# Attention in-projection of a hybrid attention and convolution block: chunk by chunk, or in pairs by Strassen's seven products

## The chip, the core and the metric

The kernel runs on one core of a Trainium2 chip. The metric is the device time of one execution in microseconds (us); lower is better. The times given are medians of several executions. Traces are taken by the hardware profiler on one execution. Engines are called as the profile calls them: PE (TensorE, matrix products; PEld its weight loads), DVE (VectorE), ACT (ScalarE), POOL (GpSimd), SP (SyncE, which here only issues transfers).

## What is computed

Two layers over 1024 latent tokens of width 1024, with a context of 256 tokens; everything is fp32. Layer 0 is attention, layer 1 a convolution module, and a final RMS norm follows. The change is in layer 0 alone:

```python
h = modulate(rmsnorm(x), shift, scale)             # (1024 tokens, 1024); h_ctx likewise (256, 1024)
proj = h @ w_in                                    # w_in (1024, 5120)
q = apply_rope(split_heads(proj[..., :2048], 16))  # 16 query heads of 128
k = apply_rope(split_heads(proj[..., 2048:2560], 4))
v = split_heads(proj[..., 2560:3072], 4)           # 4 key and value heads
z = proj[..., 3072:]                               # gate, 16 x 128
kv_c = h_ctx @ w_in[:, 2048:3072]                  # context keys and values
o = windowed_attention(q, k, v, kc, vc, sink)      # |i-j| <= 128, plus all context keys, one softmax
x = x + gate * ((o * silu(z)) @ w_out)
```

## The kernel before

**Products of split numbers.** An fp32 operand is split in a high part that TensorE's fast fp32 form takes (`F32R`; an ACT copy makes it) and a low part, the rest (one subtraction, `split_lo`, on DVE or POOL). Each product is three matmuls: high with high, high with low, low with high. Activations `Hh`, `Hl` hold the transposed `h` in 8 pages of 128 x 1024 each (8 blocks of 128 input channels, 1024 tokens). A weight chunk is 128 output columns of `w_in`, so one head of q, k, v or z: `wraw` (512 KB) is loaded, ACT makes `whi`, DVE or POOL makes `wlo`.

**The fill.** A chunk is 2 halves of 512 tokens x 8 channel blocks x 3 = 48 matmuls of 512 columns, into a bank `psg` (`gemm_half`). In the attention stage these are the fill between the attention's own matmuls. The stage goes through 128 steps: 16 heads h of 8 query blocks qb of 128 tokens. A step issues on PE the scores of the next block (6 matmuls into `pss`), `FILL = 12` fill matmuls, at some steps a product with the values (`pv`, into `pso`), and the transposes of the block's probabilities (`pss<-ident,p`). The softmax goes DVE (mask and maximum, a custom instruction), ACT (exp), DVE (reciprocal), POOL (scaling) and back to PE's transposes; ACT and DVE then split the transposed block into `pthi` and `ptlo`. Chunks for z and q are made one head ahead; every fourth head `job(("k", g))` and `job(("v", g))` run as a whole between two heads. Each chunk's result is finished by ACT, DVE and POOL: q and k by rotary positions (`rope`: copy out, swap halves by two transfers, two products and a sum, split), v by transposes and a split, z by tanh and a product.

**Beside it.** DVE also adds up the modulation rows of the second layer (`ada_rest`: `dww_raw`, `wsum_raw`, 128 transfers of 128 KB). `low_parts` makes the low parts of both output weights (ACT `lhi`, POOL `low`) and keeps them in DRAM (`wolA`, `wolC`); the projection after the attention (`proj_attn`, 32 steps of a 512 KB weight piece) loads `wo` and `wolA`.

**What sets the order.** PE goes in program order (`pin("P")`). The order on DVE, ACT, POOL and SP is set by the scheduler from priorities and its own estimate of times; each engine then runs its list in order, so that an instruction that waits holds all behind it. Transfers are issued by SP, the two of a rope swap by ACT; eight semaphores for transfers are used in turn, so that a transfer may wait for the one eight before it. Memory is 45 pages of 4 KB per partition and 6 halves of 528 words.

All instructions pass through one helper, so that every row of the trace has line L89 (after the change L144); tiles tell them apart.

```python
        for kt in range(KT):                       # gemm_half: one half of the tokens of one chunk
            PE.matmul(o, wh[:, kt], Hh[kt][:, sl], start=kt == 0, stop=False)
            yield
            PE.matmul(o, wh[:, kt], Hl[kt][:, sl], start=False, stop=False)
            yield
            PE.matmul(o, wl[:, kt], Hh[kt][:, sl], start=False, stop=kt == KT - 1)
            yield
...
        if nxt and not regroup:                    # a step of the attention stage
            scores(*nxt)
...
            fill(n)
        if pvq:
            pv(*pvq.popleft())
...
        transposes(h, qb)
```

Of the kernel before, what the change touches and what calls it, by code (L numbers as in the profile page):

```python
# [2 lines left out]

# [30 lines left out]
FILL = 12  # L34
# [42 lines left out]


# [16 lines left out]
def backbone_kernel(  # L95
# [19 lines left out]
    pg = Pages(pgpool, 45, "page", 1024)  # L115
    hp = Pages(hfpool, 6, "half", 528)

# [162 lines left out]
    for key, src in (("k", 0), wk[0]), (("q", 0), wcol(0)), (("v", 0), wv[0]):  # L280
        add_chunk(key, src)
    for h in range(NH):
        add_chunk(("z", h), wcol(AW + 2 * KW + h * P))
        if h + 1 < NH:
            add_chunk(("q", h + 1), wcol((h + 1) * P))
        if h % 4 == 3 and h + 1 < NH:
            add_chunk(("k", h // 4 + 1), wk[h // 4 + 1])
            add_chunk(("v", h // 4 + 1), wv[h // 4 + 1])
    wsA = WStream(chunks, nraw=4, lo_eng=lambda i: V if i < 4 else G)
# [375 lines left out]
    def ada_rest():  # L665
# [8 lines left out]
        bank = ps_o(1)  # L674
        acc, o = bank[:, 0:256], bank[:, 256:512]
        for i, (l, c0, kt) in enumerate(todo):
# [11 lines left out]
            yield  # L688
            if kt < KT - 1:
                continue  # L690
            V.tensor_copy(acc_a, acc)
            yield "copied"
            if i + 1 == len(todo):
                yield
            if c0 >= 2048:
                PE.matmul(o[0:1], ones[:, 0:1], acc_a, start=True, stop=True)
                V.tensor_copy(acc_a[0:1], o[0:1])
                SY.dma_start(out=gd[l][:, c0 - 2048:c0 - 1792], in_=acc_a[0:1])
            else:
                for b in range(2):  # L700
                    PE.matmul(o[:, b:b + 1], acc_a[:, b * P:b * P + P], ones[:, 0:1], start=True, stop=True)
                V.tensor_copy(mod1[:, c0 // P:c0 // P + 2], o[:, 0:2])

# [6 lines left out]
    wolA, wolC = (dr.tile([2, NK, P, 2, 512], F32, tag=n, name=n) for n in ("wolA", "wolC"))  # L710
# [5 lines left out]
    made = []  # L716

    def store():
        while made:
            dst, raw = made.pop()  # L720
            SY.dma_start(out=dst, in_=raw)
            pg.free(raw)

    def low_parts():

        items = [(pair_rows(w, m, kk), d[m, kk]) for w, d in ((Wo, wolA), (Wp, wolC)) for m in range(2) for kk in range(NK)]
        his = pg.alloc(F32R, [2, 512], "lhi")
        raws = {}

        def load(i):  # L730
            if i < len(items):
                raws[i] = pg.alloc(F32, [2, 512], "low")
                SY.dma_start(out=raws[i], in_=items[i][0])

        for i, (_, dst) in enumerate(items):
            load(i)
            raw = raws.pop(i)
            store()
            yield "open"
            for b in range(2):  # L740
                after(act(his[:, b], raw[:, b], AF.Copy), anchor_a)
                after(split_lo(G, raw[:, b], raw[:, b], his[:, b]), anchor_p)
                if b == 0:
                    yield "open"
            made.append((dst, raw))
            yield "shut"
        store()
        pg.free(his)
# [5 lines left out]
    def proj_attn():  # L754
# [4 lines left out]
        def load(i):  # L759
            s, kk = seqB[i]  # L760
            h, m = subs[s]
            w, wl = pg.alloc(F32, [2, 512], "wo"), pg.alloc(F32R, [2, 512], "wol")
            SY.dma_start(out=w, in_=pair_rows(Wo, m, kk))
            SY.dma_start(out=wl.bitcast(F32), in_=wolA[m, kk])
            st[i] = [w, wl]
# [5 lines left out]
        def split(i):  # L771
            s, kk = seqB[i]
            h, m = subs[s]
            w, wl = st[i]
            wh = pg.alloc(F32R, [2, 512], "woh")
            if i:
                act(wh, w, AF.Copy)
            else:
                V.tensor_copy(wh, w)
            pg.free(w)  # L780
# [135 lines left out]
    def early_proj():  # L916
        pg.free(*Hh, *Hl, cos, sin)
        for v in projA:
            if v == "early":
                break  # L920
            yield

    kvt = {}
    qt = {}
    zt = {}
# [12 lines left out]
    def rope(o, sl, d, ropes=None, hold=None, eng=G):  # L938
        qe, qs = (hp.alloc(F32, None, "rope") for _ in range(2))
        m = (hp if ropes is None else pg).alloc(F32, None, "rope")  # L940
        e, w, r = qe[:, 0:512], qs[:, 0:512], m[:, 0:512]
        act(e, o, AF.Copy)
        queue = A if ropes is None else SY
        queue.dma_start(out=w[0:64], in_=e[64:128])
        queue.dma_start(out=w[64:128], in_=e[0:64])
        first = tt(V, r, o, cos[:, sl], ALU.mult)
        if ropes is None:
            tt(G, w, w, sin[:, sl], ALU.mult)

        def sine():  # L950
            tt(V, w, w, sin[:, sl], ALU.mult)
            tt(V, r, r, w, ALU.add)

        def high_low():
            act(d[0][:, sl], r, AF.Copy)
            low()

        def add(behind=None):
            i = tt(eng if ropes is None and hold is None else V, r, r, w, ALU.add)
            if behind:  # L960
                after(i, [behind])
            act(d[0][:, sl], r, AF.Copy)

        def low():
            split_lo(eng if ropes is None else V, d[1][:, sl], r, d[0][:, sl])
            hp.free(qe, qs)
            (hp if ropes is None else pg).free(m)
# [1008 lines left out]
```

## Time and profile before

| | |
|---|---|
| time, median of 3 executions | 1686.36 us (1686.04 to 1686.93) |
| span of the profiled execution, first to last instruction | 1684.8 us, 1.6 us under the median; its own time is taken as the span and these 1.6 us |
| instructions | 23963 |
| PE / DVE / ACT / POOL busy | 1675.0 / 1116.1 / 878.8 / 871.0 us |
| attention stage, from the first softmax to the early output projection | 75 us to about 795 us |
| convolution layer and end | from about 960 us |
| transfers | 244.55 MB, 145 GB/s in the mean |

How to read it: "busy" is time in which an engine has an instruction of the program in work; matmuls overlap their ends, so that a busy PE says that it was never without one, and how long one matmul keeps the next from starting is read from the distance of two starts. A row of a table of stretches gives, for a window of the span, the busy time and the number of instructions of each engine, the granted clock, the mean share in which the 16 transfer engines were busy, and GB/s. A row of a group gives count, busy time, mean length of one in ns, the idle time ahead of them and what ended it.

### The profile page before, as it was taken

How to read it: one execution, taken by the hardware profiler on the slowest of the kernel's cores; microseconds unless marked ns; L12 is line 12 of the kernel's file. 1: busy time of each engine (PE TensorE's matmuls, PEld its weight loads, DVE VectorE, ACT ScalarE, POOL GpSimd, SP SyncE). 2: the span in 40 equal slices, each digit the busy share in tenths (PEclk: the TensorE clock that was granted, in tenths of full speed). 3: DMA queues.
4: the chain of work that ended last, by engine and by line, in shares of the span. 5: the costliest groups of instructions: out<-in, count | busy, mean ns of one | idle time of the engine just before them, and what ended most of it. 6: DMA issues, size and time to landing. Idle time of an engine off the chain costs nothing.

```text
span 1684.8 us, 23963 instructions
## 1 busy us (share of the span) xinstructions
PE 1675.0 (99%) x8436; PEld 1413.9 (84%) x8436; DVE 1116.1 (66%) x2131; ACT 878.8 (52%) x1555; POOL 871.0 (52%) x722
## 2 busy tenths in 40 slices
PE   9999999999999999999999999999999999999998
PEld 6888888888888888888888888888888888888886
DVE  5765654566356644566324289999999999868732
ACT  5745543555355543556334365555665654566741
POOL 0256653666366663653001267999898888130400
PEclk9999999999999999999999999999999999999999
DMA  9424443454244443447976522020211202387881
GB/s 387 150 85 153 134 121 95 153 153 141 84 152 144 143 135 98 135 135 251 320 233 228 213 94 91 11 72 17 75 51 51 82 33 80 130 276 241 310 298 50
DMA packets 114776, 244.55 MB, mean 145 GB/s; under 512 B 11626, under 2 KB 36514, under 8 KB 114656
## 3 DMA queue, kind: packets, MB, share of 16 engines
q1 hardware_dynamic: 108576, 233.06, 40.9%
q10 hardware_dynamic: 6080, 9.97, 2.4%
q8 instruction: 66, 1.08, 0.3%
q14 instruction: 54, 0.44, 0.1%
HBM read 190.80 MB, written 41.69 MB: 138 GB/s over the span
## 4 chain that ended last, share of the span: by engine, by line
PE 98%; DVE 0%; DMA 0%; ACT 0%; POOL 0%; issue 0%; ACTq 0%; POOLq 0%
PE psg L89 51%; PE pss L89 26%; PE pso L89 22%; DMA rope_half<-rope_half 0%; POOL rope_half L89 0%; DVE x_page L89 0%; ACT p_page L89 0%; DVE wlo_page L89 0%; ACT pthi L89 0%; ACT rope_half L89 0%; ACT whi_page L89 0%; DVE hf_page L89 0%; DVE hl_page L89 0%; ACT qh_page L89 0%; ACT lhi_page L89 0%
## 5 line engine op out<-in xcount | busy, mean ns | idle before, releaser
L89 POOL TENSOR_TENSOR odd_half<-odd_half,prod_half 128x513 f32<-128x513 f32 (+2 forms) x252 | 314.7, 1257 | 22.6 <-ACT prod_half L89 9.4
L89 POOL TENSOR_TENSOR wlo_page<-wraw_page,whi_page 128x512 fp32r<-128x512 f32 (+1 forms) x104 | 173.0, 1680 | 186.7 <-DVE ql_page L89 72.0
L89 PE MATMUL psg<-hh_page,whi_page 128*128 128x512 f32 x600 | 236.3, 394 | 0.0
L89 PE MATMUL psg<-hl_page,whi_page 128*128 128x512 f32 x600 | 234.4, 391 | 0.0
L89 PE MATMUL psg<-hh_page,wlo_page 128*128 128x512 f32 x600 | 234.0, 390 | 0.0
L89 ACT ACTIVATE prod_half<-ubuf,dww 128x513 f32<-128x513 f32 (+2 forms) x252 | 165.6, 675 | 116.9 <-POOL odd_half L89 113.0
L89 PE MATMUL psg<-h2h_page,whi_page 128*128 128x512 f32 x464 | 181.9, 392 | 0.0
L89 PE MATMUL psg<-h2h_page,wlo_page 128*128 128x512 f32 x464 | 180.6, 389 | 0.0
L89 PE MATMUL psg<-h2l_page,whi_page 128*128 128x512 f32 x464 | 180.6, 389 | 0.0
L89 POOL TENSOR_SCALAR p_page<-p_page,sc 128x640 f32<-128x640 f32 (+1 forms) x128 | 99.6, 779 | 149.5 <-DVE sc L89 131.8
L89 DVE SCALAR_TENSOR_TENSOR pss<-ubuf,dww,pss 128x512 f32<-128x512 f32 (+3 forms) x270 | 172.4, 670 | 0.1
L89 DVE SCALAR_TENSOR_TENSOR pss<-ubuf,wsum,pss 128x512 f32<-128x512 f32 (+3 forms) x270 | 171.7, 671 | 0.2
L89 ACT ACTIVATE p_page<-p_page,sc 128x641 f32<-128x641 f32 (+1 forms) x128 | 102.9, 804 | 98.3 <-DVE sc L89 95.9
L89 ACT ACTIVATE pthi<-pss 128x512 fp32r<-128x512 f32 (+2 forms) x144 | 87.3, 618 | 109.7 <-PE pss L89 99.8
L89 DVE TENSOR_TENSOR ptlo<-pss,pthi 128x512 fp32r<-128x512 f32 (+2 forms) x144 | 101.8, 716 | 61.2 <-ACT pthi L89 59.9
L89 PEld LDWEIGHTS psg<-hh_page,wlo_page 128*128 128x128 f32 x600 | 112.7, 188 | 24.3
L89 PEld LDWEIGHTS psg<-hh_page,whi_page 128*128 128x128 f32 x600 | 112.8, 188 | 19.2 <-ACT hh_page L89 0.3
L89 PEld LDWEIGHTS psg<-hl_page,whi_page 128*128 128x128 f32 x600 | 112.8, 188 | 18.4
L89 ACT ACTIVATE whi_page<-wraw_page 128x1024 fp32r<-128x1024 f32 x88 | 92.6, 1052 | 49.8 <-PE psg L89 21.1
L89 PE MATMUL pso<-h2h_page,whi_page 128*128 128x512 f32 x304 | 118.3, 389 | 0.0
L89 PE MATMUL pso<-h2h_page,wlo_page 128*128 128x512 f32 x304 | 118.3, 389 | 0.0
L89 PE MATMUL pso<-h2l_page,whi_page 128*128 128x512 f32 x304 | 118.3, 389 | 0.0
(262 smaller groups left out, 3992.4 us busy)
## 6 DMA issues: line engine op xcount, KB each, us to landing
wraw_page<-in_k_wconv_dram SPq DMA_DIRECT2D x48, 512.0 KB, 3.3
wraw_page<-in_k_win_dram SPq DMA_DIRECT2D x40, 512.0 KB, 3.6
wo_page<-in_attn_w_out_dram SPq DMA_DIRECT2D x32, 512.0 KB, 6.2
wol_page<-wolA SPq DMA_DIRECT2D x32, 512.0 KB, 8.3
wo_page<-in_conv_w_out_dram SPq DMA_DIRECT2D x32, 512.0 KB, 6.7
wol_page<-wolC SPq DMA_DIRECT2D x32, 512.0 KB, 6.2
rope_half<-rope_half ACTq DMA_DIRECT2D x76, 128.0 KB, 2.4
araw_page<-in_k_ada_dram SPq DMA_DIRECT2D x16, 512.0 KB, 10.1
```

Of the source, the lines that this page charges most:

```text
L89: r = f(*a, **k)
```

## The change

36 of the 40 chunks are now made in 18 pairs (`pairs`: q and z of heads 1 to 15, k and v of groups 1 to 3; q, k, v and z of head or group 0 stay as they were). For a pair, the 1024 channels are two halves, the 1024 tokens two halves, and the two chunks the two column halves of a 2 x 2 block product, which Strassen's scheme (Winograd's form) makes with seven block products in place of eight: 7 x 4 channel blocks x 3 = 84 matmuls in place of 96. For it

- the activations' block sums S1 to S4 are made once, in head 0, by DVE, POOL and ACT (`sums`). S3 takes the place of the block of tokens 512 to 1023 in channels 0 to 511 in `Hh`, `Hl`; S4 stays in memory (`s4`); S1 and S2 go to DRAM (`sd`) and are streamed in for each pair, 8 loads of 512 KB (`sw`, from `stream`, each issued as PE has used the block that it replaces);
- the weights' block sums are made for each pair by DVE: 4 subtractions of 128 x 512; high parts are 7 ACT copies, low parts 7 subtractions, 3 on DVE (`PAIR_V`) and 4 on POOL;
- the products go to three banks (`psg`, `pso`, `psg`) that the pairs share; ACT copies one of them to start the next sum (`pso<-psg`) and two out, and 4 DVE sums put the results together. Of one of the halves q's or k's input now comes from memory and not from PSUM; the gate of both halves and the cosine product likewise.

With it the surroundings move: gates go to DRAM and back (`zd`), keys and values of groups 1 to 3 too (`kd`, `vd`, `cd`), so that no chunk is made as a whole between two heads; the context's chunks are all made in head 0; cosine and sine are loaded anew for each half (`k_cos`, `k_sin`); q is allocated by halves; `ada_rest` adds up in memory and not in PSUM. `low_parts` makes only `wolC`; `proj_attn` makes the low parts of its weights itself, by POOL (`wol<-wo,woh`). Small transfers and splits are put off by a count of fill matmuls (`soon`), and `quota` says how many fill matmuls lie behind each step: 258 in head 0, then 14, 13.1, 13.1 and 10.5 a step in the four groups.

```diff
-FILL = 12
+KEPT = 12
+ROPE_AT = 12
+HEAD0 = (30, 36, 36, 36, 36, 28, 28, 28)
+PAIR_V = (1, 4, 6)
...
-    wsA = WStream(chunks, nraw=4, lo_eng=lambda i: V if i < 4 else G)
+    wsA = WStream(chunks, nraw=4, lo_eng=lambda i: V if i < 4 or i % 2 else G)
...
+        def halves(self, src, i, b, then=None):
+            t = pw[0].alloc(F32R, [2, 512], "whl")
+            act(t[:, 0], src, AF.Copy)
+            def low():
+                split_lo(V if b in PAIR_V else G, t[:, 1], src, t[:, 0])
...
+            if b == 0:
+                self.halves(r1[:, 0], i, b)
+                self.t[i] = t = pw[0].alloc(F32, [2, 512], "wt")
+                tt(V, t[:, 0], r2[:, 1], r2[:, 0], ALU.subtract)
+            elif b == 1:
+                t = self.t[i]
+                self.halves(t[:, 0], i, b)
+                tt(V, r2[:, 0], r2[:, 0], r1[:, 0], ALU.subtract)
+                tt(V, t[:, 1], r2[:, 1], r2[:, 0], ALU.subtract)
+            elif b == 2:
+                self.halves(r1[:, 1], i, b)
+                tt(V, r1[:, 0], r1[:, 1], self.t[i][:, 1], ALU.subtract)
...
+    ORDER = ("A11", "S3", "A12", "S2", "A22", "S4", "S1")
+    STREAM = ("S2", "S1")
+    def sums(k):
+        f, g = (pg.alloc(F32, [2, 512], "sf") for _ in range(2))
+        for t, i, eng in ((f, k, V), (g, k + 4, G)):
+            tt(eng, t.rearrange("p a b -> p (a b)"), Hh[i].bitcast(F32), Hl[i].bitcast(F32), ALU.add)
+        yield
+        tt(V, g[:, 1], f[:, 1], g[:, 1], ALU.add)
+        tt(V, f[:, 1], f[:, 0], f[:, 1], ALU.subtract)
+        tt(V, f[:, 0], g[:, 1], f[:, 0], ALU.subtract)
+        tt(V, g[:, 0], g[:, 0], f[:, 0], ALU.subtract)
...
+        for n, src in (("S3", f[:, 1]), ("S2", f[:, 0]), ("S4", g[:, 0]), ("S1", g[:, 1])):
+            hi, lo = dst[n]
+            split_lo(G if n == "S1" else V, lo, src, hi)
...
+    def job_pair(i):
...
+        for b, n in enumerate(ORDER):
+            bank, first = ((a_, True), (c_, True), (a_, False), (b_, False), (a_, True), (b_, False), (c_, True))[b]
+            w = wsP.need(7 * i + b)
+            for k in range(4):
+                ah, al = hblock(n, k)
+                for p, (x, y) in enumerate(((w[0], ah), (w[0], al), (w[1], ah))):
+                    PE.matmul(bank, x[:, k], y, start=first and k == 0 and p == 0, stop=k == 3 and p == 2,
+                              skip_group_check=not first)
+                    yield
+                hdone(i, n, k)
...
+            if b == 0 and i:
+                act(b_, a_, AF.Copy)
+            if b == 1:
+                act(zs, c_, AF.Copy)
+            if b == 3:
+                tt(V, zs, b_, zs, ALU.add)
+            if b == 4:
+                tt(V, e, a_, zs, ALU.add)
+        act(e0, c_, AF.Copy)
+        tt(V, e1, e0, zs, ALU.add)
+        tt(V, e0, b_, e0, ALU.add)
```

**PE, in a step of head 1.** Of the kernel before, the fill: one chunk (`whi`, `wlo`) with the activations' pages, at the end of one half of the tokens and the start of the other.

```order
L89 MATMUL psg_1455<-hh_page_546,whi_page_1339 128x512
L89 MATMUL psg_1455<-hl_page_547,whi_page_1339 128x512
L89 MATMUL psg_1455<-hh_page_546,wlo_page_1340 128x512
L89 MATMUL psg_1551<-hh_page_268,whi_page_1339 128x512
L89 MATMUL psg_1551<-hl_page_269,whi_page_1339 128x512
L89 MATMUL psg_1551<-hh_page_268,wlo_page_1340 128x512
```

Of the changed kernel, from the last row of a score product: the streamed block sums S2 with the weights of one product (`whl` holds its high and its low part), and the next product.

```order
L144 MATMUL pss_2281<-kvc_page_616,q_page_1942 128x256
L144 MATMUL pso_1482<-sw_page_2079,whl_page_2173 128x512 x3
L144 MATMUL pso_1482<-sw_page_2111,whl_page_2173 128x512 x3
L144 MATMUL psg_1481<-hh_page_410,whl_page_2189 128x512
L144 MATMUL psg_1481<-hl_page_411,whl_page_2189 128x512
L144 MATMUL psg_1481<-hh_page_410,whl_page_2189 128x512
L144 MATMUL psg_1481<-hh_page_449,whl_page_2189 128x512
```

A matmul of the fill has the same shape as before, and there are fewer; some now read what a transfer has just brought, and all read weights that were made for one product.

**DVE, in head 0, ahead of the third softmax.** Of the kernel before, between two softmax instructions (`ISA p_page`), with the two evictions of the first block's results:

```order
L89 ISA p_page_959,sc_960<-pss_952,mask_page_597,nsink 128x640
L89 ISA sc_960 128x1
L89 TENSOR_TENSOR rope_half_899<-pss_621,cos_page_560 128x512
L89 SCALAR_TENSOR_TENSOR zs_page_915<-zs_page_915,psg_918 128x512
L89 RECIPROCAL sc_960<-sc_960 128x1
L89 TENSOR_TENSOR ptlo<-pss_988,pthi 128x4x128
L89 SCALAR_TENSOR_TENSOR pso_945<-dww_raw,cs,pso_945 128x256
```

Of the changed kernel, the same place:

```order
L144 ISA p_959,sc_960<-pss_952,mask_page_597,nsink 128x640
L144 ISA sc_960 128x1
L144 TENSOR_TENSOR wlo_page_1034<-wraw_page_972,whi_page_1033 128x1024
L144 TENSOR_TENSOR sf_page_1198<-hh_page_343,hl_page_344 128x1024
L144 TENSOR_TENSOR hl_page_269<-sf_page_1044,hh_page_268 128x512
L144 RECIPROCAL sc_960<-sc_960 128x1
L144 SCALAR_TENSOR_TENSOR zs_half_979<-zs_half_979,psg_919 128x512
L144 TENSOR_TENSOR sf_page_1105<-hh_page_300,hl_page_301 128x1024
L144 TENSOR_TENSOR wlo_page_1167<-wraw_page_1040,whi_page_1166 128x1024
```

The block sums (`sf`, and S3's low part into `hl`) and the context weights' low parts (`wlo`) now stand between the softmax's instructions; all of them have two inputs in memory.

**SP, in the middle of the attention.** Of the kernel before:

```order
L89 DMA wsum_raw<-in_ada_w_dram 128x256
L89 DMA ozd<-oz_half_1374 128x384
L89 DMA dww_raw<-in_ada_w_dram 128x256
L89 DMA low_page_1508<-in_attn_w_out_dram 128x2x512
L89 DMA wsum_raw<-in_ada_w_dram 128x256
L89 DMA dww_raw<-in_ada_w_dram 128x256
L89 DMA wolA<-low_page_1387 128x1024
```

Of the changed kernel:

```order
L144 DMA sw_page_5501<-sd 128x1024
L144 DMA wsum_raw<-in_ada_w_dram 128x256
L144 DMA rope_half_5423<-oz_page_5312 64x512 x2
L144 DMA ozd<-oz_page_5460 128x384
L144 DMA sw_page_5513<-sd 128x1024
L144 DMA sw_page_5547<-sd 128x1024
L144 DMA sw_page_5552<-sd 128x1024
L144 DMA cos_page_5715<-in_k_cos_dram 128x512
L144 DMA cos_page_5715<-in_k_sin_dram 128x512
```

The stream's blocks (`sw`), the swaps of late halves (`rope`, 64 partitions each), cosine and sine now stand in SP's list with the modulation rows and the stores; in all SP's list has 1022 transfers, before 654.

721 lines of the change are left out of this document (499 added, 222 removed).

## Prediction

> **What bounds the kernel now.** I read the page's busy times and the chain that ended last first, then a table of stretches for the stage that the change touches, then PE's own timeline there.
>
> ```profile
> span 1684.8 us, 23963 instructions
> PE 1675.0 (99%) x8436; PEld 1413.9 (84%) x8436; DVE 1116.1 (66%) x2131; ACT 878.8 (52%) x1555; POOL 871.0 (52%) x722
> PE 98%; DVE 0%; DMA 0%; ACT 0%; POOL 0%; issue 0%; ACTq 0%; POOLq 0%
> ```
>
> PE is never without a matmul but for 9.8 us, and 98% of the chain is its. So what counts is how long matmuls keep each other from starting, and whether anything new makes PE wait. The stretches (columns: PE, PEld, DVE, ACT, POOL busy, granted clock, share of the transfer engines, GB/s), the attention stage first, then one group of four heads (heads 4 to 7), then three stretches with heavy transfers:
>
> ```profile
> 75.00:795.00 720.00, 719.90 (x4001) 627.08 (x4000) 402.98 (x898) 361.92 (x774) 401.95 (x366) 1.00 0.43 134
> 264.30:452.70 188.40, 188.40 (x1056) 165.50 (x1056) 103.89 (x230) 93.67 (x201) 108.75 (x98) 1.00 0.44 133
> 800.00:900.00 100.00, 100.00 (x464) 82.83 (x463) 31.58 (x69) 33.27 (x48) 6.48 (x13) 1.00 0.81 280
> 810.00:850.00 40.00, 40.00 (x189) 32.83 (x188) 8.66 (x20) 15.29 (x20) 3.53 (x10) 1.00 0.95 332
> 820.00:840.00 20.00, 20.00 (x90) 16.58 (x89) 5.34 (x9) 7.96 (x12) 2.51 (x2) 1.00 1.00 376
> ```
>
> In 720 us of attention stage PE idles 0.1 us, DVE is 56% busy, ACT 50%, POOL 56%, transfers 43%: PE alone is the bound, and each other engine has room. The price of a fill matmul is the distance of starts, not the 390 ns that a group's mean shows. One step's fill of twelve, first and last, and the transpose behind:
>
> ```profile
> 301.09 0.40 PE L89 MATMUL psg<-hh_page,whi_page 128*128 128x512 f32 x1
> ...
> 303.61 0.39 PE L89 MATMUL psg<-hh_page,wlo_page 128*128 128x512 f32 x1
> 303.84 0.27 PE L89 MATMUL pss<-ident,p_page 128*128 128x128 f32 x1
> ```
>
> Twelve take 303.84 - 301.09 = 2.75 us, 0.229 us each.
>
> **The change, part by part.**
>
> *PE.* 18 pairs lose 12 matmuls each, 216; one added to clear a bank: 215 x 0.229 = 49.2 us. All else on PE keeps its count and shapes. Without a wait the stage takes 671 us in place of 720, and the whole span 1635.6; with the 1.6 us around it 1637.2, set against the median of 1686.4. The rest of this part asks what fills up meanwhile.
>
> The prices on the other engines:
>
> ```profile
> L89 DVE TENSOR_TENSOR rope_half<-psg,cos_page 128x512 f32<-128x512 f32 x36 | 24.8, 690 | 23.1 <-ACT rope_half L89 22.0 <-ACT p_page L89 0.8
> L89 DVE TENSOR_TENSOR rope_half<-rope_half,rope_half x9: 679/693/1769, 238.4 to 624.5; 128x512 f32<-128x512 f32 x9
> L89 DVE TENSOR_TENSOR rope_half<-rope_half,rope_half 128x512 f32<-128x512 f32 x9 | 9.4, 1047 | 14.0 <-POOL rope_half L89 14.0
> 15.52 1.22 DVE L89 TENSOR_TENSOR wlo_page<-wraw_page,whi_page 128x1024 fp32r<-128x1024 f32 x1
> L89 POOL TENSOR_TENSOR wlo_page<-wraw_page,whi_page 128x512 fp32r<-128x512 f32 x72 | 93.1, 1315 | 120.3 <-DVE ql_page L89 72.0 <-PE pso L89 18.6 <-ACT whi_page L89 16.8
> L89 ACT ACTIVATE lhi_page<-low_page 128x512 fp32r<-128x512 f32 x64 | 40.1, 626 | 0.0
> L89 ACT ACTIVATE rope_half<-psg 128x512 f32<-128x512 f32 x36 | 21.3, 591 | 18.7 <-PE psg L89 18.3
> L89 ACT ACTIVATE whi_page<-wraw_page 128x1024 fp32r<-128x1024 f32 x88 | 92.6, 1052 | 49.8 <-PE psg L89 21.1 <-issue 12.9 <-DMA wraw_page<-in_k_win_dram 6.7
> ```
>
> A 128 x 512 operation of DVE takes 0.69 us, if one input is in PSUM always; with both in memory the nine rope sums have a median of 693 ns, a mean of 1047 and a maximum of 1769. The long ones began under a POOL operation:
>
> ```profile
> 248.71 2.99 POOL L89 TENSOR_TENSOR wlo_page<-wraw_page,whi_page 128x512 fp32r<-128x512 f32 x2
> 248.79 1.76 DVE L89 TENSOR_TENSOR rope_half<-rope_half,rope_half 128x512 f32<-128x512 f32 x1 [0.26 <-POOL rope_half L89]
> ```
>
> DVE started 0.08 us behind POOL's first subtraction and ended after 1.76 us in place of 0.69; POOL's two took 2.99 in place of 2 x 1.315. [...]
>
> *DVE.* Per pair 4 weight differences, 3 low parts and 4 output sums: 11 x 0.69 = 7.6 us, 137 in 18 pairs. The block sums: 4 x (one of 1024 at 1.22 and seven of 512) = 24. Three more context low parts of 1024, 4. Less 12 special rope operations and 16 copies, 15. 403 + 150 = 553 of 671 us, 82%. New with both inputs in memory are, per pair, 7 of the weights, one sum, two gates, two cosine products, 12; with the block sums' 28 and the three, 247. At the mean of 1047 they add 247 x 0.354 = 87: 640 us, 95%. DVE then has room on the average and hardly any in a stretch.
>
> *POOL* gives up 66 weight low parts and 32 of the output weights' and takes 72 low parts and 8 block sum operations (four of double width): 402 - 87 - 42 + 95 + 16 = 384, 57%; that pays for itself. *ACT*: 126 high parts at 0.63 for 36 chunks at 1.05, 41 more; 54 bank copies at 0.6, 32 more; 16 sums, 10; less 32 `lhi`, 18 rope copies and 16 gate copies, 37: 408, 61%. No cost, with the room that POOL and ACT have, unless they stand behind a late DVE.
>
> *Transfers.* Stream 144 x 0.52 MB = 75.5, its stores 4, gates out and in 19, cosine and sine 17, keys, values and context 16, less `low` and `wolA` of the first output weight 17: 115 MB on the 96 of the stage (720 us x 134 GB/s), 211 MB in 671 us, 315 GB/s. A group of four heads (188.4 us now, about 169 without five pairs' 60 matmuls and the context chunk) needs 56 MB by SP's list, 330 GB/s. That is the rate of 810 to 850, where the engines were 0.95 busy and PE never waited; 820 to 840 shows 376 at 1.00. A streamed block is asked for 36 fill matmuls ahead, about three steps of 5 us; landings were
>
> ```profile
> wraw_page<-in_k_win_dram SPq DMA_DIRECT2D x40, 512.0 KB, 3.6
> wol_page<-wolA SPq DMA_DIRECT2D x32, 512.0 KB, 8.3
> ```
>
> 3.6 us in the light attention stage and 8.3 in the heavy one behind it. 15 us cover 8.3; a kv pair's stretch (25 MB in 68 us, 370 GB/s) uses the reserve up. Bounds 0 and, at 332 GB/s, 25 / 0.332 - 68 = 7 us in each of three regroups, 22. I take 4, nearer the 376 row.
>
> ```profile
> 289.45 0.28 PE L89 MATMUL pso<-pthi,vh_page 128*128 128x256 f32 x1
> 289.56 0.28 PE L89 MATMUL pso<-ptlo,vh_page 128*128 128x256 f32 x1
> 289.68 0.28 PE L89 MATMUL pso<-pthi,vl_page 128*128 128x256 f32 x1
> ```
>
> *Head 0.* Here the block sums, the context's six chunks and the first weights meet. From the first softmax of head 0 to the low part of the second product's weights DVE's list has 84 operations: 37 with two inputs in memory (31 x 0.69 + 6 x 1.22 = 28.7) and 47 others, 22: 51 us, to 64 if the 37 cost 0.354 more each. PE has 42.5 us there: 66 matmuls at 0.229, 168 of 256 columns at 0.12 (the distance of the starts below), and 60 small ones for the rest. PE must wait for that low part: 51 less overlapping ends is 48, so 5 us at least, 21 at most. With POOL busy for just over half of that time I take 10.
>
> *The other heads.* The softmax of a step goes through DVE, ACT, DVE, POOL, and PE needs it a step later:
>
> ```profile
> 333.53 0.87 DVE L89 CUSTOM_DVE_ANT_0 p_page<-pss,mask_page,nsink 128x640 f32<-128x640 f32 x1
> 336.51 0.80 POOL L89 TENSOR_SCALAR p_page<-p_page,sc 128x640 f32<-128x640 f32 x1
> 339.38 0.71 PE L89 MATMUL pss<-ident,p_page 128*128 128x128 f32 x5
> ```
>
> POOL ended at 337.31, PE asked at 339.38: 2.1 us to spare at 55% DVE. Behind one DVE operation that is blocked (1.07 us more) the room holds; behind two it doesn't. Bounds 0 and 2 us a head; with 82 to 95% busy and room of 2 us I take 0.5 in each of 15 heads, 7.
>
> *The output projection.* The `wol` loads go, and POOL makes 62 subtractions of 1.3 us where it has 6.48 of 100 us busy (800 to 900). Per weight piece 1.05 + 2 x 1.3 = 3.7 us against 24 matmuls, 5.5. PE did not wait for transfers there, so nothing is gained; 0 to 5, taken as 0.
>
> *Sum:* -49 + 10 + 7 + 4 = -28 on a span of 1684.8: 1656.8, and 1658.4 as time.
>
> **Rivals.**
>
> *PE stays full.* DVE's list in head 0 starts early enough, everything else is hidden: 1637 to 1643. For it, a stretch of the convolution layer in which DVE is 98% busy and POOL 87% and PE misses nothing; against it, the 51 us of DVE beside 42.5 of PE in head 0, of which 5 must show.
>
> ```profile
> 1200.00:1400.00 200.00, 200.00 (x884) 165.62 (x883) 195.65 (x279) 119.19 (x158) 173.46 (x120) 1.00 0.17 58
> ```
>
> *DVE becomes the bound because POOL shuts it out.* With a mean of 0.693 + (671 - 553) / 247 = 1.17 us per two-input operation DVE fills the stage, and 1.37 eats the whole gain; at the largest value, 1.77, DVE needs 553 + 247 x 1.08 = 820 us, time 1786. The nine rows' mean, 1.05, stands just below the point, with POOL about as busy as it will be. [...]
>
> *Transfers set the pace (slower).* SP's list is one queue, with half as many transfers again; one that waits for PE or DVE holds the stream's loads behind it, and PE then waits for `sw`. It decides at 211 MB / 720 us = 293 GB/s: below that nothing is won. 800 to 900 ran at 280, with engines at 0.81; at that rate the stage takes 754 us, time 1720. Against it: nothing there asked for more.
>
> **How the numbers follow.** About 0.2% (3.4 us) can be told from no change: 1683.0 to 1689.8 counts as the same. The forecast (1643 to 1680) has 0.58; PE full 0.18; DVE shut out, from 1680 on, 0.11 (0.03 faster, 0.02 the same, 0.06 slower); transfers 0.13 (0.03, 0.03, 0.07). Faster 0.82, same 0.05, slower 0.13. The likeliest gives 1658; 8 in 10 lie between 1639 (nearly nothing waits) and 1690.
>
> **What would show it.** PE with about 8220 instructions and 12 to 40 us of idle time; waits of PE's `pso` in head 0 for DVE or POOL `whl`; DVE 1240 to 1350 us busy, its two-input operations at a mean of 0.8 to 1.1; POOL near 935, ACT near 925; 345 MB moved, 300 GB/s or more in the stage; nothing changed from the convolution on. PE waits for `sw` loads above 20 us, or for POOL's probabilities in each head, would prove me wrong on the slow side; no idle PE in head 0 on the fast side.

## The result: 6.9% slower, and the profile after

| | before | after |
|---|---|---|
| time, median of 4 executions | 1686.64 us | 1802.44 us |
| ratio, 95% interval | | 1.0687 (1.0672 to 1.0702) |
| span of the profiled execution | 1684.8 us | 1800.3 us |
| PE without a matmul | 9.8 us | 118.0 us |
| mean granted clock | 0.999 | 0.972 |

The head of the page and the chain that ended last:

```profile
span 1800.3 us, 24912 instructions
PE 1682.3 (93%) x8221; PEld 1400.5 (78%) x8221; DVE 1374.4 (76%) x2337; ACT 919.4 (51%) x1649; POOL 1012.5 (56%) x778
PE 62%; DVE 14%; DMA 13%; issue 4%; POOL 2%; ACT 2%; SPq 1%; ACTq 0%; DVEq 0%; POOLq 0%
```

215 matmuls are gone, as forecast, and the span grew by 115.5 us. PE's busy time is 1682.3 us where 1675.0 - 49.2 = 1625.8 were to be expected, 56.5 too much; its idle time is 108.2 above that of before: -49.2 + 56.5 + 108.2 = 115.5. The same columns as in the prediction, first the whole attention stage, then head 0, then the rest of it:

```profile
75.85:910.00 834.15, 734.83 (x3822) 621.18 (x3823) 648.34 (x1106) 404.56 (x878) 474.01 (x371) 0.94 0.78 257
78.80:168.00 89.20, 69.08 (x372) 60.09 (x371) 73.64 (x105) 38.89 (x80) 50.32 (x33) 0.84 0.62 214
168.00:910.00 742.00, 664.18 (x3446) 559.73 (x3445) 572.63 (x1000) 362.98 (x793) 420.74 (x337) 0.95 0.80 263
```

The loss lies in the attention stage: 834 us in place of 720, from 910 us on the kernel takes what it took. PE idles 20 us in head 0 and 78 in the other fifteen heads, 5.2 each in the mean. No engine is full: DVE is busy 78% of the stage, POOL 57%, ACT 48%, the transfer engines 78% at 257 GB/s. The largest of PE's waits over the whole span (in total, how often, longest):

```profile
PE pso L144 <- DVE ptlo L144: 16.4, 12, 4.0
PE pss L144 <- DVE ptlo L144: 11.6, 14, 3.6
PE pss L144 <- ACT q_page L144: 9.8, 4, 6.5
PE pss L144 <- POOL p L144: 9.5, 6, 2.9
PE pss L144 <- DVE sc L144: 9.0, 14, 1.5
```

Most are small. Somewhat under half of the 110 us that the view lists, 51 us with 4.2 for `pthi`, ends with a part of the softmax (`sc`, `p`, `pthi`, `ptlo`); the rest is scattered over q, gates and sums, and none is for a streamed block `sw`. Three waits are longer than 6 us, 19 us together, and all end with ACT: for q (6.5), for the copy of a bank (6.6) and for weights (`whl`, 6.1). They are not the softmax's. Ahead of the longest, the copy stood in ACT's list behind two others, and ACT itself had waited 2.43 us for POOL.

**One of the softmax's waits.** DVE, POOL and PE around 401 us:

```profile
400.87 1.75 DVE L144 TENSOR_TENSOR whl_page<-wt_page,whl_page 128x512 fp32r<-128x512 f32 x1
402.55 1.75 DVE L144 TENSOR_TENSOR wraw_page<-wraw_page,wt_page 128x512 f32<-128x512 f32 x1
404.22 0.81 DVE L144 TENSOR_TENSOR ptlo<-pss,pthi 128x640 fp32r<-128x640 f32 x1
400.64 1.43 POOL L144 TENSOR_TENSOR rope_half<-rope_half,cos_page 128x512 f32<-128x512 f32 x1
402.03 1.71 POOL L144 TENSOR_TENSOR whl_page<-wraw_page,whl_page 128x512 fp32r<-128x512 f32 x1
405.08 0.80 PE L144 MATMUL pso<-ptlo,ctx_half 128*128 128x512 f32 x1 [4.00 <-DVE ptlo L144]
```

A low part and a weight difference, 0.69 us each at their groups' medians, took 1.75 beside POOL's operations; POOL's low part took 1.71 where its group's median is 1.30. `ptlo` stood behind them, and PE waited 4.0 us. Over the stage, worked out from the trace's rows, 401 DVE operations have two tensors in memory (23 before), and they take some 128 us more than at the median of those that met no POOL operation. (The forecasts of e1 and e3 say 354 and 113: that count leaves out 47 whose two inputs lie in tiles of one name.) POOL's scaling of the probabilities takes 0.94 us in place of 0.78.

**What a wait costs beyond itself.** Two waits, of 6.56 and 2.30 us, in windows of 2 us, and PE's rows at their ends and two from the slow stretch behind the first:

```profile
362.00:364.00 2.00, 0.71 (x4) 0.23 (x2) 2.00 (x5) 0.33 (x3) 2.00 (x2) 1.00 1.00 401
366.00:368.00 2.00, 0.00 (x0) 0.00 (x0) 1.50 (x3) 0.41 (x1) 0.76 (x2) 0.86 0.28 94
370.00:372.00 2.00, 2.00 (x7) 1.54 (x6) 1.97 (x4) 1.75 (x3) 1.25 (x1) 0.50 0.00 0
374.00:376.00 2.00, 2.00 (x12) 1.84 (x11) 1.00 (x2) 1.31 (x4) 0.36 (x1) 0.93 0.92 324
780.00:782.00 2.00, 0.12 (x1) 0.00 (x0) 2.00 (x5) 1.60 (x3) 2.00 (x2) 1.00 0.77 287
784.00:786.00 2.00, 2.00 (x8) 2.00 (x8) 1.95 (x3) 0.00 (x0) 1.20 (x2) 0.50 0.22 66
```

```profile
369.27 0.80 PE L144 MATMUL psg<-hh_page,whl_page 128*128 128x512 f32 x1 [6.56 <-ACT oz_page L144]
782.42 0.50 PE L144 MATMUL pso<-ptlo,ctx_half 128*128 128x512 f32 x1 [2.30 <-DVE ptlo L144]
370.29 1.06 PE L144 MATMUL psg<-hh_page,whl_page 128*128 128x512 f32 x2
371.14 0.63 PE L144 MATMUL psg<-hl_page,whl_page 128*128 128x512 f32 x1
```

The granted clock is the third number from the end. By the clock's record in the trace it falls to 0.50 at 367.4 us, in PE's wait of 6.56 us, and is back at 374.3, 5 us after that wait; meanwhile two fill matmuls take 371.14 - 370.29 = 0.85 us, 0.43 each in place of 0.23. The record shows 19 such stretches in the stage, 3.4 to 10.2 us long, 99 us together. PE was busy for 83 of them, and half of that, 41 us, is most of PE's 56.5 us too much. (A further 10 us, by an estimate, are the ends of the last matmuls ahead of the stage's 63 waits, which no next matmul overlaps: 0.39 - 0.23 us each.) In the changed kernel, in its sixteen variants below and in e14, PE's busy time grew by 0.38 to 0.55 of what was added to its idle time, 0.52 here. So a lost microsecond of waiting cost about half a microsecond more, most of it by the clock.

### The profile page after: what moved, and what is told of

Its sections match the earlier page's. It is cut to its first block, busy times and chain, and to the rows that moved or that the text cites. A ratio compares the mean times of both kernels' runs of the same rounds, so it can differ in the third digit from the quotient of the medians.

```text
span 1800.3 us, 24912 instructions
## 1 busy us (share of the span) xinstructions
PE 1682.3 (93%) x8221; PEld 1400.5 (78%) x8221; DVE 1374.4 (76%) x2337; ACT 919.4 (51%) x1649; POOL 1012.5 (56%) x778
## 3 DMA queue, kind: packets, MB, share of 16 engines
q8 instruction: 65, 1.06, 0.2%
## 4 chain that ended last, share of the span: by engine, by line
PE 62%; DVE 14%; DMA 13%; issue 4%; POOL 2%; ACT 2%; SPq 1%; ACTq 0%; DVEq 0%; POOLq 0%
PE psg L144 27%; PE pso L144 18%; PE pss L144 17%; DMA wraw_page<-in_k_win_dram 3%; DMA sw_page<-sd 2%; DVE mask_page L144 2%; DVE ptlo L144 2%; DVE p L144 2%; DVE sf_page L144 1%; DMA dww_raw<-in_ada_w_dram 1%; DMA rope_half<-rope_half 1%; DVE oz_page L144 1%; DMA wo_page<-in_attn_w_out_dram 1%; DVE wraw_page L144 1%; SPq L144 1%
## 5 line engine op out<-in xcount | busy, mean ns | idle before, releaser
L144 POOL TENSOR_SCALAR p<-p,sc 128x640 f32<-128x640 f32 (+1 forms) x128 | 120.8, 944 | 188.7 <-DVE sc L144 122.6
L144 PE MATMUL psg<-hh_page,whl_page 128*128 128x512 f32 x576 | 193.4, 401 | 7.3 <-ACT oz_page L144 6.6
L144 ACT ACTIVATE p<-p,sc 128x641 f32<-128x641 f32 (+1 forms) x128 | 102.9, 804 | 137.9 <-DVE sc L144 122.4
L144 POOL TENSOR_TENSOR wlo_page<-wraw_page,whi_page 128x1024 fp32r<-128x1024 f32 (+1 forms) x38 | 88.8, 2341 | 115.0 <-ACT whi_page L144 77.6
L144 PEld LDWEIGHTS psg<-hh_page,whl_page 128*128 128x128 f32 x576 | 109.9, 194 | 29.0 <-ACT oz_page L144 7.0
L144 ACT ACTIVATE woh_page<-wo_page 128x1024 fp32r<-128x1024 f32 x63 | 66.6, 1057 | 107.6 <-DMA wo_page<-in_conv_w_out_dram 44.8
L144 PE MATMUL pss<-kh_page,q_page 128*128 128x384 f32 (+1 forms) x256 | 97.8, 382 | 23.4 <-ACT q_page L144 9.8
L144 PE MATMUL psg<-hl_page,whl_page 128*128 128x512 f32 x288 | 115.4, 401 | 0.0
L144 PE MATMUL pss<-ident,p 128*128 128x128 f32 x608 | 90.3, 278 | 22.8 <-DVE ptlo L144 11.2
L144 POOL TENSOR_TENSOR wol_page<-wo_page,woh_page 128x512 fp32r<-128x512 f32 x62 | 83.2, 1365 | 50.2 <-ACT woh_page L144 26.7
## 6 DMA issues: line engine op xcount, KB each, us to landing
araw_page<-in_k_ada_dram SPq DMA_DIRECT2D x16, 512.0 KB, 10.2
```

Source lines behind the costliest of these rows:

```text
L144: r = f(*a, **k)
```

## The experiments

Each ran once, with a profile, beside the kernel before (1685.5 to 1687.0 us). The changed kernel's four executions lie between 1801.1 and 1804.3, so differences under 3 us are not read.

**Lock, stream and the sharing out of work (e1 to e4).** "Lock" is short for what the rows at 400.87 show: DVE operations with two inputs in memory took 1.75 us in place of 0.69 beside POOL operations that read memory, one of which took 1.71 in place of 1.30. e1 turns `tt(V, out, a, b, op)` into a form with one tensor:

```diff
-tt(V, t[:, 0], r2[:, 1], r2[:, 0], ALU.subtract)
+V.tensor_scalar(out=t[:, 0], in0=r2[:, 1], scalar1=r2[:, 0, 0:1], op0=ALU.subtract, op1=ALU.add, accum_out=sink1, ...)
... (likewise the other new ones)
```

> The changed kernel with its new DVE operations on two tensors in memory (weight differences, DVE's low parts, block sums, the modulation rows, cosine product, gate, one output sum; about 330 of the stage's 354) replaced by operations of the same size on one tensor and a column of the other, which also read out an accumulator; values are wrong, PE's, ACT's and POOL's work and all transfers stay. Theory L (DVE and POOL shut each other out of memory; 113 us of DVE in the attention stage and what follows from it): the 512-column operations come down from a mean of 986 ns to about 0.75 us, PE's idle time from 118 to below 50 us, the clock from 0.972 to 0.99 or more, the time to 1660 to 1710. Rival D (DVE's list is too full and badly ordered, the lock adds little): above 1770. Rival T (transfers): above 1770, PE idle above 90.

Measured 1758.65: 44 us off, although the one-tensor form adds a read of the accumulator, 81 ns in the trace, to each operation. The weight differences take 0.74 us in place of 0.95 to 1.06, PE's idle time is 90.7, the clock 0.978. The lock is a real cause and not the only one; the forecast of theory L was far too good.

```diff
-        SY.dma_start(out=t.bitcast(F32), in_=sd[a, k])        # stream
-            t = win[(n, k)]
+            t = s4[k]                                          # hblock, S1 and S2
```

> The changed kernel without the 144 loads of streamed block sums (75 MB): S1's and S2's products read S4, which lies in memory; values are wrong, all else stays. Theory T (transfers at 257 GB/s make loads, rotary swaps and the softmax's neighbours late): PE's idle time falls from 118 to below 60, time below 1740. Theory L (DVE against POOL): at most 20 us less, 1780 to 1800, since DVE and POOL do what they did. Rival D: the same as L.

1786.09: 16 us off, with 75 MB fewer to move. The amount that the stream moves is no main cause.

```diff
-G.tensor_scalar(out=p[:, 0:w], in0=p[:, 0:w], scalar1=ri, scalar2=1.0, op0=ALU.mult, op1=ALU.mult)
+act(p[:, 0:w], p[:, 0:w], AF.Copy, scale=ri)
```

> The changed kernel with the scaling of the probabilities (128 operations of POOL, 0.95 us each in the stage, 120 us) done by ACT. Same values. Theory L: a quarter of POOL's reads is gone, so a quarter of the 113 us of DVE's lengthening too, and the softmax has one engine change less behind POOL's queue: 1750 to 1785. Rival D: DVE's list is as long as before, 1790 to 1810. Rival A (ACT, in whose queue the splits stand behind what waits, becomes the late one): above 1810.

1796.22: 6 us off, PE idle 112.1. DVE's busy time falls by 24 us. That the scaling now stands in ACT's list behind the splits may be why so little is gained; no run shows it.

```diff
-PAIR_V = (1, 4, 6)
+PAIR_V = ()
```

> The changed kernel with all seven low parts of a pair's weights on POOL (three of them were DVE's): DVE loses 54 operations of 128x512 on two tensors, POOL gains 54 at 1.4 us. Rival D (DVE's list too full): DVE has 54 us less to do, so 1750 to 1780. Theory L: the exclusive time is DVE's two-tensor time and POOL's time added; 54 x 0.7 less on one side and 54 x 1.4 more on the other, so no faster, 1795 to 1830.

1799.90, within the noise of no change, as L said. That what DVE gives up comes back on POOL's side is L's reading of it. e12, which moves another product the same way, agrees:

```diff
-tt(V, e, e, ct, ALU.mult)
+tt(G, e, e, ct, ALU.mult)
```

> The changed kernel with the cosine product of the rotary halves (about 36 operations on two tensors in memory that stand behind a load) on POOL in place of DVE; same values. Theory W: DVE then has no instruction that waits for cosine, 1770 to 1790. Theory L: the product takes 1.3 us of POOL for 0.7 of DVE and still shuts the other out: 1795 to 1810.

1798.02, 4 us off and in L's range. Work moved between DVE and POOL gains next to nothing.

**A thin DVE list (e5, e6, e8 to e10).** e5 leaves out the pairs' arithmetic on DVE and the additions of modulation rows:

```diff
-                tt(V, t[:, 0], r2[:, 1], r2[:, 0], ALU.subtract)      # and the three others
-                split_lo(V if b in PAIR_V else G, t[:, 1], src, t[:, 0])
+                if b not in PAIR_V: split_lo(G, t[:, 1], src, t[:, 0])
-                after(stt(acc, raw, cs[:, kt:kt + 1], acc, ALU.mult, ALU.add))
+                pass
```

> The changed kernel without the pairs' weight differences and DVE's three low parts (126 operations of 128x512) and without 112 of the 128 additions of modulation rows (their loads stay); matmuls read the high parts instead, values are wrong. DVE has about 140 us less work and some 60 us less waiting for POOL. Theory Q (the softmax's three DVE instructions of each step stand in DVE's list behind other work, so every us of that list is paid, whatever makes it long): waits between the softmax's parts come down to nearly those of before, PE idle below 60 us, time 1680 to 1720. Theory O (the list's order is at fault, not its length): above 1750. Theory T (transfers and SP's order): above 1760.

1750.09, with DVE at 471 of 780 us, 60%: 52 us off, and still 63 above the kernel before. Theory Q in this form falls. One thing that held PE there is seen in DVE's and PE's rows:

```profile
204.85 0.69 DVE L144 SCALAR_TENSOR_TENSOR oz_half<-pso,zl_half 128x512 f32<-128x512 f32 x1 [9.38 <-DMA zl_half<-zd]
205.46 0.81 DVE L144 TENSOR_TENSOR ptlo<-pss,pthi 128x640 fp32r<-128x640 f32 x1
206.41 0.74 PE L144 MATMUL pss<-ident,p 128*128 128x128 f32 x5 [2.75 <-DVE ptlo L144]
```

DVE stood idle 9.38 us before a gate that comes back from DRAM, with `ptlo` behind it. The gates were in memory before the change.

> The one-tensor DVE operations and the missing stream loads together. Alone they took 44 and 16 us off. If the two causes are separate: about 1742. If PE's waits have one cause in the softmax's chain, to which each adds, and the clock falls with each long wait: 1715 to 1735. If transfers are what is left after the lock (T): below 1715.

1729.88. With most of the lock gone the stream is worth 29 us, not 16: the causes cover each other, and the differences here can't be added up.

> The thin DVE list of the other kernel and no stream loads. Theory Q: 5 to 15 us under the thin list alone, 1675 to 1705, with head 0 still long (its block sums stay). Theory T: over 20 us under it. Theory O: above 1735.

1752.95, the same as with the stream.

```diff
-        w, ct, st = (hx.alloc(n) for n in ("rope", "cos", "sin"))
+        w, ct, st = hx.alloc("rope"), cos[:, 0:512], cos[:, 0:512]    # no loads; gates likewise
```

> The thin DVE list, and besides no loads of cosine, sine and gates in the attention stage: DVE and POOL read a table that stays in memory (wrong values); swaps, stores and the stream stay. In the thin kernel DVE waited 80 us for transfers in the attention stage (before the change 2.5), one of them 9.4 us for a gate with the softmax behind it. Theory W (a DVE instruction that waits for a load holds the softmax behind it in the list): 1690 to 1720, DVE's waits for transfers below 45 us. Theory O (the order of the list is at fault wherever the data lie): 1735 to 1755.

1733.51: 17 us under e5, between the two forecasts. e10 leaves out the block sums' arithmetic and the stream as well:

> Everything that was suspected is left out together: the thin DVE list, resident cosine, sine and gates, no block sums in head 0 (copies by ACT in their place), no stream loads; PE's 8221 matmuls stay. Theories Q and W together (length of DVE's list, lock, waits for loads) say that PE's saving then shows: 1640 to 1665, PE idle below 25 us, clock 0.995 or more. If the way in which the pairs share three banks or the order of the lists held PE: above 1690.

1733.84, no less. The waits in SP's own list, two of e10 and one of the changed kernel, suggest why:

```profile
SPq L144 <- DMA wsum_raw<-in_ada_w_dram: 88.5, 50, 4.1
SPq L144 <- DMA dww_raw<-in_ada_w_dram: 76.1, 39, 8.7
SPq L144 <- DVE mask_page L144: 75.1, 53, 5.7
```

Where nobody adds up the modulation rows, their loads follow each other at once, and each waits in SP's list for the one ahead, with weights behind it. So e5, e8, e9 and e10, which all have these unread loads, may stand higher than they should. By how much is open: in the changed kernel the same rows hold SP's list too, there for DVE's additions (75.1 us).

**Head 0 alone (e11)**, without the block sums' arithmetic, with copies by ACT in its place:

> The changed kernel without the arithmetic of the block sums in head 0 (32 DVE and POOL operations on two tensors; ACT copies activations in their place, which are then stored, loaded and multiplied as before; wrong values). Head 0 took 89 us, 20 of them without PE. If the block sums are what keeps DVE there: head 0 at 68 to 74 us, time 1780 to 1788. If the context's weights and first pair's weights hold it as well: head 0 above 80, time above 1792.

1783.77, head 0 at 72.0 us in place of 89.2. The block sums cost 17 to 19 us, nearly all of it in head 0.

**Order (e7, e16).** e7 pins DVE to program order and puts the reciprocal five matmuls later; e16 wraps the softmax's instructions in the scheduler's high priority.

> The changed kernel with DVE's instructions of the attention stage in program order in place of the scheduler's, and the reciprocal and the scaling put five fill matmuls behind the exponential's issue; same work, same values. In program order a step's maximum stands right behind the scores' issue and the split of the transposed block right behind the transposes. Theory O: waits ahead of the maximum and of the low split shrink, time 1720 to 1770. Theory Q: the work ahead of them only changes places, 1780 to 1840.

1852.23: 50 us worse, beyond both forecasts. So the order matters much, and the scheduler's is the better of these two.

> The changed kernel with the softmax's instructions (maximum, exponential, reciprocal, scaling, and the splits of the transposed block) put ahead of other work wherever the scheduler has a choice; same work, same values. Theory O: 1740 to 1780. Theory Q/W: the lists are as long and what is late stays late, 1790 to 1810.

1796.33: 6 us off. A much better order was not found, which does not say that there is none.

**DVE's load on the kernel before (e14, e15).** Two idle operations in each attention step, 253 in all, on two tensors or on one:

```diff
+tt(V, mask[:, 0:512], mask[:, 0:512], mask[:, 0:512], ALU.max)                                       # e14
+V.tensor_scalar(out=mask[:, 0:512], in0=mask[:, 0:512], scalar1=-3.0e38, op0=ALU.max, op1=ALU.max, accum_out=sink1, ...)  # e15
```

> The kernel before with two idle DVE operations more in each attention step (about 250 of 128x512 on two tensors in memory, 0.69 us or more each, that nobody waits for; same values): DVE's load of the changed kernel and the lock with POOL without anything else of the change. Theory Q with L (length of DVE's list and the lock are enough): PE idle above 50 us, time above 1740. Theory W/O (it takes the pairs' tight dependences and late loads): below 1710.

> The kernel before with the same two operations more in each step, on one tensor with an accumulator read out, so that POOL is not shut out: the length of DVE's list without the lock. Theory L: 1686 to 1695, while the two-tensor one is far above. Theory Q: within 15 us of the two-tensor one. Theory W/O: both below 1710.

1715.23 and 1689.08. The groups of the idle operations of e14, then of e15, and POOL's scaling in both:

```profile
L89 DVE TENSOR_TENSOR mask_page<-mask_page 128x512 f32<-128x512 f32 x253 | 242.0, 957 | 3.1
L89 POOL TENSOR_SCALAR p_page<-p_page,sc 128x640 f32<-128x640 f32 x96 | 90.8, 946 | 139.0 <-DVE sc L89 119.8 <-PE pss L89 13.8 <-DMA low_page<-in_conv_w_out_dram 1.8
```

```profile
L89 DVE TENSOR_SCALAR_CACHE_REDUCE mask_page<-mask_page 128x512 f32<-128x512 f32 x253 | 171.9, 679 | 3.1
L89 DVE DVE_READ_ACCUMULATOR mask_page<-mask_page 128x1 f32 x253 | 20.7, 82 | 0.0
L89 POOL TENSOR_SCALAR p_page<-p_page,sc 128x640 f32<-128x640 f32 x96 | 77.1, 804 | 130.0 <-DVE sc L89 108.6 <-PE pss L89 19.1 <-DMA low_page<-in_conv_w_out_dram 1.8
```

POOL's 804 is what it took in the kernel before (806). The stretch from 75 to 795 us of e14, then of e15, then of the changed kernel, for comparison:

```profile
75.00:795.00 720.00, 702.53 (x3845) 607.00 (x3844) 586.75 (x1100) 342.82 (x744) 444.96 (x358) 0.99 0.40 123
```

```profile
75.00:795.00 720.00, 718.00 (x3982) 624.36 (x3982) 546.24 (x1389) 359.68 (x770) 401.13 (x365) 1.00 0.43 134
```

```profile
75.00:795.00 720.00, 634.93 (x3305) 538.77 (x3306) 561.06 (x957) 349.06 (x764) 417.00 (x322) 0.94 0.79 263
```

This pair is the clearest of the study. DVE 76% busy leaves PE with 718 of 720 us where the added work has one input and nobody waits for it; in the changed kernel DVE is 78% busy and PE has 635. So the length of DVE's list alone is not the cause. Nor are length and lock together: in e14 DVE is 81% busy, more than in the changed kernel, and PE has 702.5; at 1715.23 e14 lies between its two forecasts, nearer to that of theory W/O. The lock is worth 26 us where nothing else is changed: 957 ns in place of 679 for DVE, 946 in place of 804 for POOL's scaling. In the changed kernel other work waits for the added operations, and they wait for transfers themselves; in this pair neither is so.

**What is left (e13, e17, e18).** e13 is e10 without the 112 unread loads, e17 also without the rotary swaps (`queue.dma_start(out=w[0:64], in_=e[64:128])` and its twin), e18 also with one-tensor forms for DVE's remaining two-tensor operations.

> The light kernel, and of the modulation rows also no loads (112 of 128 are left out), so that SP's list is not held by loads that nobody reads: in the light kernel SP waited 165 us for those loads, and ACT 80 us for weights behind them. Theory W (what is late on the loaded lists holds the softmax): 1650 to 1690, PE idle below 35 us. Theory O (the order of the lists, made by a scheduler whose times are not the chip's): 1715 to 1740.

1703.62, 30 us off, between the two forecasts. Of what remained, DVE's and PE's rows near 300 us:

```profile
295.29 1.55 DVE L144 TENSOR_TENSOR rope_half<-rope_half,cos_page 128x512 f32<-128x512 f32 x1 [2.54 <-DMA rope_half<-rope_half]
296.83 1.70 DVE L144 TENSOR_TENSOR stage_page<-rope_page,stage_page 128x512 f32<-128x512 f32 x1
299.86 0.67 DVE L144 TENSOR_TENSOR ptlo<-pss,pthi 128x512 fp32r<-128x512 f32 x1
300.59 0.80 PE L144 MATMUL pso<-ptlo,kvc_page 128*128 128x512 f32 x1 [2.85 <-DVE ptlo L144]
```

DVE waited 2.54 us for the swap, and then took 1.55 and 1.70 us for operations with two inputs in memory, more than twice the 0.69 us that such rope sums had as their median in the kernel before; all this stood ahead of `ptlo`. The cosine product `tt(V, e, e, ct)` overwrites what the swap's transfer still reads; before the change it read PSUM, wrote elsewhere and waited for no transfer.

> The light kernel without modulation rows, and without the rotary swaps' transfers (POOL multiplies the half itself in place of the swapped copy; wrong values). Theory W: DVE and POOL have no late transfer left in front of the softmax, 1650 to 1680, PE idle below 30 us. Theory O (the order of the lists): 1690 to 1710.

> The same, and DVE's remaining two-tensor operations of the stage (cosine products, one output sum, the gate, context low parts) on one tensor. If the lock adds on top even here: 5 to 25 us below the kernel without swaps, 1640 to 1665. If only waits for transfers and the order were left: within 5 us of it.

1677.72 and 1672.47: 26 us for the swaps, 5 for the last of the lock. e18's engines, and its stretch over heads 1 to 10:

```profile
PE 1635.6 (98%) x8221; PEld 1377.7 (82%) x8221; DVE 1127.3 (67%) x2162; ACT 925.0 (55%) x1661; POOL 931.4 (56%) x770
```

```profile
146.80:580.60 433.80, 431.20 (x2382) 375.37 (x2381) 245.92 (x590) 249.66 (x550) 257.68 (x235) 1.00 0.34 114
```

Here PE is nearly as full as it was before the change (99.4% of the stretch), at full clock. e18's span is 1670.6 = 1684.8 - 49.2 + 25.2 (more idle time, 35.0 - 9.8) + 9.8 (PE busy longer, some 7.6 of it at half clock). PE's saving is real; what was left out costs, together, 130 us. How much each part takes in the full kernel stays open, since they cover each other: e1 with e2 gave 73 us where singly they gave 60. Of the versions that compute the reference none beat the kernel before.

## Why the prediction was wrong, point by point

The waits ahead of the softmax's three DVE instructions, means over 119 of the 128 steps in us, worked out from starts and ends in each trace (good to about 0.1 us, by how the rows of a step are matched):

| | before | e15 | e14 | after | e18 |
|---|---|---|---|---|---|
| scores' end to maximum | 0.66 | 0.81 | 1.16 | 2.04 | 0.74 |
| exponential to reciprocal | 0.15 | 0.49 | 0.93 | 1.03 | 0.27 |
| high part to low part | 0.26 | 0.32 | 0.58 | 1.22 | 0.37 |
| scores' end to scaled probabilities | 4.28 | 4.90 | 5.89 | 6.97 | 4.72 |
| kernel's time | 1686.6 | 1689.1 | 1715.2 | 1802.4 | 1672.5 |

- *PE's saving*, 49 us: right. PE has 8221 instructions, and in e18, where it waits little, its busy time is within 9.8 us of the expected 1625.8, the half clock included.
- ***The other heads*, 7 us: the step that failed.** It was 78 us of idle time, and the clock took 31 of its 41 us there. The spare of 2.1 us was read from one step. A step passes DVE three times, each pass now waits about 1 us longer, and the chain's growth from 4.28 to 6.97 us is more than the spare. The bounds, "0 and 2 us a head", took one blocked operation as the rule; the row at 400.87 shows two in a row ahead of `ptlo`. And the step had no term for an operation that waits for a transfer or for another engine's list with the softmax behind it: that e14, with the load and the lock, lost 29 us and the changed kernel 116 suggests that much of the loss lies there, or in the order of the lists. How it is shared out is open.
- *Clock: no term at all.* The traced stage before held 1.00, and I let every wait cost only itself. In the trace after, the clock stood at 0.50 for 99 us of the stage in all; it fell in the wait of 6.56 us and behind that of 2.30 us at 780 us, and PE was busy some 41 us longer for it.
- *DVE*: 1374 us where 1240 to 1350 were forecast, 648 in the stage against 640. That the two are near is in part luck. 247 new operations with both inputs in memory were counted. (That sum counts gates for the three k and v pairs, which have none, and leaves out four block sums of double width; the two slips nearly cancel.) But the modulation rows' additions, 111 of 256 columns and 30 of 128, had moved from PSUM into memory and were not counted; on the other side, the 246 operations of 512 columns took in the mean 0.29 us more than alone, not 0.354. The groups of the 111:

```profile
L144 DVE SCALAR_TENSOR_TENSOR mask_page<-wsum_raw,cs,mask_page 128x256 f32<-128x256 f32 x63 | 52.2, 828 | 1.9 <-DMA wsum_raw<-in_ada_w_dram 1.6
L144 DVE SCALAR_TENSOR_TENSOR mask_page<-dww_raw,cs,mask_page 128x256 f32<-128x256 f32 x48 | 35.4, 738 | 10.8 <-DMA dww_raw<-in_ada_w_dram 10.8
```

They take 0.83 and 0.74 us; those that met no POOL operation have a median of 0.475, and in the kernel before, with one input in PSUM, the mean was 0.48.
- *Rival "DVE becomes the bound because POOL shuts it out"* (0.11): the right engine, priced by the wrong measure. It asked for a mean of 1.37 us before the gain is gone, when DVE has no idle time left. The 246 operations of 512 columns had a mean of 0.98, DVE idled 22% of the stage, and the loss was already more than twice the gain. Its largest case, 1786 us, comes near the measured time by luck: there DVE is full. A late list needs no full engine.
- *POOL*, 935 forecast, 1012 measured: its operations took longer too (the scaling 0.94 us in place of 0.78), which I had priced for DVE alone. With DVE's one-tensor forms, in e1, POOL's time is 951.
- *Transfers*, 4 us: PE waits for no streamed block, as forecast, and the stage ran at 257 GB/s. That transfers could delay DVE was missed: DVE waited 2.5 us for transfers in the stage before, and 50 after, with the softmax's instructions in the same list. All of before, then the largest of after:

```profile
DVE pso L89 <- DMA dww_raw<-in_ada_w_dram: 2.1, 2, 1.5
DVE pso L89 <- DMA wsum_raw<-in_ada_w_dram: 0.4, 1, 0.4
```

```profile
DVE mask_page L144 <- DMA dww_raw<-in_ada_w_dram: 10.8, 6, 5.1
DVE rope_half L144 <- DMA rope_page<-rope_half: 8.5, 3, 4.3
DVE wt_page L144 <- DMA wraw_page<-in_k_win_dram: 7.7, 6, 3.7
```

- *Head 0*, 10 us with 21 as the upper bound: 20 us of idle time, and the clock of 0.84 there costs some 9 more (PE was busy for 19 us at half clock). By e11 the block sums are more than half of these 29 us.
- *The output projection*, 0: right; the time behind the stage is that of before.

## What to carry to other kernels

Where a short chain passes through an engine's in-order list several times per step, price each added instruction by what stands behind it, and not by the engine's mean load: DVE at 76% cost 2 to 3 us (e15), at 81% and with the lock 29 (e14), and at 78% in the changed kernel 116, where DVE also waited for transfers and others waited for it. An operation that reads two tensors in memory beside a busy POOL (957 ns in e14, with one tensor 679 in e15), or whose input comes back from DRAM (DVE idle for 9.38 us in e5), is a possible stall for everything behind it, so ask that of every operand that an edit moves from PSUM or from memory. And if PE is to wait at all, add about half again, most of it for the clock: all 18 traces with such waits show 0.38 to 0.55.

## What the runs showed of the hardware

- Half clock was seen at short waits of PE too: one of 2.30 us (at 780.1, with one of 0.78 five us earlier) was followed by 3.4 us of it, and in the second of two close together, 1.03 and 1.47 us (at 439.9 and 441.7), the clock fell for 6.8 us. A wait of 2.00 us at 578.9 was not followed by any, so in this trace the length of a wait alone does not tell.
- The lock between DVE and POOL, measured by itself (e14 and e15): a DVE operation of 128 x 512 took 679 ns with one tensor and 957 with two, and POOL's one-tensor scaling went from 804 to 946 ns.
